# Channel-mixer weight tiles of a two-layer streaming encoder: split up-weights and first and third block sums placed 64 bytes further in longer tiles

## The chip, the core and the metric

The kernel runs on one core of a Trainium2 chip. The metric is the device time of one launch in microseconds (us): the median of several executions, lower is better. A profiled execution on the same core gives the trace from which all shares and durations below come.

## What is computed

The reference is a two-layer encoder over 512 tokens of width 1024 in float32. Layer 0 mixes the tokens with a matrix memory (four heads) and with cross-attention to 256 memory tokens; layer 1 mixes them with chunked band attention (twelve heads) and again with cross-attention. What matters here is the channel mixer that follows in each layer, a gated multilayer perceptron with a causal depthwise convolution of width 3 on its gate, inner width 2816 (22 tiles of 128):

```python
def conv_ffn(h, w_up, conv_w, conv_b, w_down):
    u, g = jnp.split(h @ w_up, 2, axis=-1)
    g = causal_dwconv(g, conv_w, conv_b)
    return (jax.nn.silu(g) * u) @ w_down
...
        x = x + conv_ffn(rmsnorm(x, norm_ffn_g[l]), ffn_w_up[l], ffn_conv_w[l], ffn_conv_b[l], ffn_w_down[l])
```

## The kernel before, in words

Float32 products are made of three matmuls in the float32r type. Every operand is split into a high part (ScalarE, `A.copy`, line 130) and a low part (VectorE, source minus high part, line 131); `mm3` (lines 167 to 171) then multiplies high by high (line 169), high by low (line 170) and low by high (line 171) into one PSUM accumulator. Each of the three is one weight load of 128 by 128 and one matmul over the columns of the other operand. Within `mm3` the stationary operand, the one that is loaded as weights, is mostly a slice of a split weight tile; only the value columns and the last products of the kernel have a split weight tile as the moving operand.

Split weights lie in two rings of three tiles each, `wh` for the high parts and `wl` for the low parts, 128 partitions by 1024 elements (4096 bytes a partition). `parts` (line 148) takes one tile of each ring and splits a raw tile into them; `halves` (line 155) takes the tiles alone. The raw weights come by DMA into the ring `wr`, or, for the gate's weights, into one of two large `pt` tiles. Activations, the split "forms" of this text and much else lie in 57 tiles of 2048 bytes, the ring `u`.

In the program as built, the tiles of `u`, `pt`, `wr`, `t`, `wh` and `wl` all begin 64 bytes past a multiple of 2048 bytes in their partition. A slice of 128 weights takes 512 bytes, and slices of activations begin at halves of their tile (0 or 1024 bytes). So, with a few exceptions, every weight load and every moving operand begins 64 bytes past a multiple of 512. One exception is used below: the value columns of layer 0 (`value_columns(1)`, lines 979 to 1008, called in line 1220) have a moving operand of 392 columns, whose second half begins at 392 times 4 bytes, 32 bytes further with respect to 512. Another is the all-ones weight tile `onesr` (line 103), which begins 128 bytes past a multiple of 512.

A channel mixer (`ChannelMixer`, line 640) does its first five tiles plainly (`plain`, line 676). Its `later` (line 787) does the other 17 in steps that are written out by hand under a manual schedule for TensorE, ScalarE and VectorE (`step`, line 808). A step multiplies 256-column halves of the activations by blocks of the up and gate weights and by sums of such blocks, a scheme that saves block products. The weights of step j+1 are prepared by the class `Forms` (line 854) while step j runs: `sums` and `sum_third` make the block sums in the large tile `mixer.s`, `split_up` (line 889) splits the up weights into `a11` and `a12`, and `split_sums` (line 892) splits the first and third sums into `s1` and `s3`; these two call `parts` and so use `wh` and `wl`. `split_second`, `split_gate` and `split_fourth` put the second sum, a gate block and the fourth sum into `u` tiles; `split_down` (line 899) uses `parts` for the down weights.

In a step, `self.products` (line 766) with `a11`, `a12` and `s1` (lines 828, 831, 839) issues 12 matmuls of 256 columns each. `s3` is used in line 843: in the 12 wide steps of a mixer (j from 9 to 20) by `wide_products` (lines 780 to 785), four pairs of a 256-column matmul with the low part (line 784) and a 512-column matmul with the high part (line 785); in the other five steps by `products`, 12 matmuls of 256 columns. A step's down products (lines 741 to 748) are 512 columns wide and also use `wh` and `wl`.

The order on every engine is the program's: the manual schedule fixes the steps, and the rings `wh` and `wl`, three deep, decide when a split may overwrite an old tile.

Of the kernel before, what the change touches and what calls it, by code (L numbers as in the profile page):

```python
# [10 lines left out]
F32R = mybir.dt.float32r  # L11
# [5 lines left out]
P = 128  # L17
D = 1024
# [37 lines left out]
def trunk(  # L56
# [30 lines left out]
    def sb(tag, shape, dtype=F32):  # L87
        count[0] += 1
        return pool.tile(shape, dtype, tag=tag, name=f"{tag}{count[0]}", bufs=bufs[tag])

    def ps(tag):
        count[0] += 1
        return psum.tile([P, S], F32, tag=tag, name=f"p{tag}{count[0]}", bufs=pbufs[tag])
# [35 lines left out]
    def split(hi, lo, src, on_act=True, pinned=False):  # L129
        high = A.copy(hi, src) if on_act else V.tensor_copy(hi, src)  # L130
        low = V.tensor_tensor(out=lo, in0=src, in1=f(hi), op=ALU.subtract)  # L131
        if pinned:
            pin(high)
            pin(low)
# [10 lines left out]
            nc.sync.dma_start(raw[:, :, b:], extra)  # L145
        return raw

    def parts(raw, pinned=False):
        _, a, b = raw.shape
        hi = sb("wh", [P, D], F32R)[:, : a * b].rearrange("p (a b) -> p a b", a=a)  # L150
        lo = sb("wl", [P, D], F32R)[:, : a * b].rearrange("p (a b) -> p a b", a=a)
        split(hi, lo, raw, pinned=pinned)
        return hi, lo

    def halves(raw):

        _, a, b = raw.shape
        return [sb(tag, [P, D], F32R)[:, : a * b].rearrange("p (a b) -> p a b", a=a) for tag in ("wh", "wl")]

    def weights(*args):  # L160
        return parts(load(*args))

    def rows(w, c0, n, k0=0, k1=None):
        k1 = k1 if k1 is not None else w.shape[0] // P
        return w[k0 * P : k1 * P, c0 : c0 + n].rearrange("(k p) c -> p k c", p=P)
# [85 lines left out]
    class Norm:  # L251
# [14 lines left out]
        def finish(self):  # L266


            parts = [sb("t", [P, S], F32R) for _ in range(2)]
            split(*parts, self.acc)  # L270
            yield 7.4
            o = ps("sc")
            for i, part in enumerate(parts):
                nc.tensor.matmul(o, onesr, part, start=i == 0, stop=i == 1)
            v, r, t = sb("rb", [P, S]), sb("t", [P, S]), sb("t", [P, S])
            A.activation(t, o, AF.Ln, scale=1.0 / D, bias=eps)
            V.tensor_scalar(v, o, 1.0 / D, EPS, op0=ALU.mult, op1=ALU.add)
            A.activation(r, t, AF.Exp, scale=-0.5)
            A.activation(t, r, AF.Square)
            yield 4  # L280
            V.scalar_tensor_tensor(t, t, -0.5, v, op0=ALU.mult, op1=ALU.mult)
            self.row = sb("rb", [P, S])
            V.scalar_tensor_tensor(self.row, t, 1.5, r, op0=ALU.add, op1=ALU.mult)
# [133 lines left out]
    def value_weights(hf, u):  # L417
        n = AW // 2
        ex = rows(a_w_in, 4 * AW, 2 * AH, 2 * u, 2 * u + 2) if hf else None
        return load(rows(a_w_in, 2 * AW + hf * n, n, 2 * u, 2 * u + 2), 2, n, ex)  # L420

    with tc.manual_schedule(engines={mybir.EngineType.PE, mybir.EngineType.Activation, mybir.EngineType.DVE}):
# [9 lines left out]
        for q in range(KT // 2 + 1):  # L432
            if q < KT // 2:
# [6 lines left out]
                hi, lo = sb("u", [P, S], F32R), sb("u", [P, S], F32R)  # L440
# [32 lines left out]
        for j in range(KT):  # L473
            G.dma_start(xspill[j], xT[j])
        norm.spread()
        vws1.append(halves(vraw1[1]))
        A.copy(vws1[1][0], vraw1[1])
        vo = two_banks("mm", "sc")
        value_products(vo, *vws1[0], 0)
        keep(1, 0, ko, A.copy)  # L480
        raw = value_weights(1, 0)
        vw = [halves(raw)]
        A.copy(vw[0][0], raw)
        x_scaled(0)
# [369 lines left out]
    class Forms:  # L854
# [32 lines left out]
            self.sub(self.halves(self.s13)[1], self.halves(self.up)[0], self.halves(self.gate)[0])  # L887

        def split_up(self):
            self.a11, self.a12 = zip(*(self.halves(t) for t in parts(self.up)))  # L890

        def split_sums(self):
            self.s1, self.s3 = zip(*(self.halves(t) for t in parts(self.s13)))

        def sum_fourth(self):
            s2, s4 = self.halves(self.s24)
# [371 lines left out]
    for j in range(KT):  # L1268
        wh, wl = weights(rows(ffn_w_down[0], j * P, P, FT - LAST, FT), LAST, P)
        o = ps("mm")  # L1270
# [175 lines left out]
    for hf in range(2):  # L1446
# [6 lines left out]
        for Ts, pieces in groups:  # L1453
            for c in pieces:
                if c.start:
                    os_[Ts[0]] = ps("mm")
                for u in range(n):
# [3 lines left out]
                    wh, wl = ws[u]  # L1461
# [61 lines left out]
```

## Time and profile before

| | |
|---|---|
| median of 3 runs | 1194.86 us (1194.71 to 1195.16) |
| the profiled execution, its own time | 1195.72 us |
| its span, first to last instruction | 1194.0 us |
| TensorE matmul, busy | 1183.5 us (99%) |
| weight loads, busy (beside the matmuls) | 1037.0 us (87%) |
| VectorE, busy | 961.7 us (81%) |
| ScalarE, busy | 725.2 us (61%) |
| GpSimd, busy | 130.3 us (11%) |
| mean granted TensorE clock | 0.999 |

Matmuls are pipelined, so their durations overlap, and a busy share of 99% says only that there is hardly a moment without one. What a matmul costs is read from the timeline, as the time from one start to the next. `PE` stands for the matmuls, `PEld` for the weight loads, `DVE` for VectorE, `ACT` for ScalarE, `POOL` for GpSimd. A name such as `pmm<-u,wh` gives what is written, then the moving operand, then the weights.

### The profile page before, as it was taken

To read this page: it belongs to the slowest core of one execution; us is meant where nothing else is said; L and a number is where in the kernel's file an instruction comes from. 1 tells how busy PE (TensorE), PEld (TensorE's weight loads), DVE (VectorE), ACT (ScalarE), POOL (GpSimd) and SP (SyncE) were. 2 spreads that over 40 slices of the span, in tenths; PEclk is the share of its full clock that TensorE was granted. 3 is DMA by queue.
4 is the path that set the end of the run, shared out by engine and by line. 5 is a ranking of instruction groups with operands and counts; after the bars stand their busy time and mean duration, and the time that the engine had idled before them with its cause. 6 is when DMAs were issued, how large, how long until landed. Compare 5 with 4: busy or idle time off the path is not lost.

```text
span 1194.0 us, 18184 instructions
## 1 busy us (share of the span) xinstructions
PE 1183.5 (99%) x6719; PEld 1037.0 (87%) x6719; DVE 961.7 (81%) x1760; ACT 725.2 (61%) x1294; POOL 130.3 (11%) x222
## 2 busy tenths in 40 slices
PE   9999999999999999999999999999999999999997
PEld 9988888888899998999888888888889988999986
DVE  6877788788978888888698888997896888888855
ACT  5648677655656555555576677776565655555545
POOL 1211201010021111111020000101001011011100
PEclk9999999999999999999999999999999999999999
DMA  8645313444265676665464313246336455665551
GB/s 289 212 108 140 84 54 80 152 144 141 88 156 147 156 165 165 154 144 123 142 204 123 89 54 101 69 135 185 111 99 141 116 139 135 142 141 139 119 158 71
DMA packets 200155, 158.61 MB, mean 133 GB/s; under 512 B 8344, under 2 KB 179838, under 8 KB 200066
## 3 DMA queue, kind: packets, MB, share of 16 engines
q1 hardware_dynamic: 183906, 119.74, 34.1%
q0 software_dynamic: 15584, 36.67, 14.9%
q8 instruction: 53, 0.87, 0.3%
q10 hardware_dynamic: 576, 1.05, 0.2%
q14 instruction: 36, 0.29, 0.1%
HBM read 128.89 MB, written 32.46 MB: 135 GB/s over the span
## 4 chain that ended last, share of the span: by engine, by line
PE 92%; ACT 3%; DVE 2%; DMA 1%; SPq 1%; issue 0%; POOL 0%; POOLq 0%; DVEq 0%; ACTq 0%
PE pmm L169 15%; PE pmm L170 15%; PE pmm L171 15%; PE ptr L171 6%; PE ptr L169 6%; PE ptr L170 6%; PE pmm L785 6%; PE psc L171 5%; PE psc L170 5%; PE psc L169 5%; PE pmm L784 3%; PE psc L519 2%; PE ptr L1350 1%; DMA wr<-in_mem_w_kv_dram 1%; PE ptr L1371 1%; PE ptr L1372 1%
## 5 line engine op out<-in xcount | busy, mean ns | idle before, releaser
L169 PE MATMUL pmm<-u,wh 128*128 128x512 f32 (+1 forms) x872 | 309.1, 355 | 0.3 <-ACT u L130 0.2
L170 PE MATMUL pmm<-u,wh 128*128 128x512 f32 (+1 forms) x872 | 306.2, 351 | 0.0
L171 PE MATMUL pmm<-u,wl 128*128 128x512 f32 (+1 forms) x872 | 306.0, 351 | 0.0
L131 DVE TENSOR_TENSOR wl<-wr,wh 128x1024 fp32r<-128x1024 f32 (+3 forms) x172 | 199.8, 1163 | 57.0 <-ACT wh L130 55.0
L130 ACT CAST wh<-wr 128x1024 fp32r<-128x1024 f32 (+3 forms) x172 | 172.4, 1004 | 97.7 <-PE pmm L170 44.5
L171 PEld LDWEIGHTS pmm<-u,wl 128*128 128x128 f32 x872 | 164.5, 189 | 21.1
L169 PEld LDWEIGHTS pmm<-u,wh 128*128 128x128 f32 x872 | 164.5, 189 | 18.5 <-ACT u L130 1.1
L170 PEld LDWEIGHTS pmm<-u,wh 128*128 128x128 f32 x872 | 164.7, 189 | 18.2 <-DVE u L131 0.5
L169 PE MATMUL ptr<-u,wh 128*128 128x512 f32 x272 | 106.7, 392 | 0.0
L171 PE MATMUL ptr<-u,wl 128*128 128x512 f32 x272 | 106.1, 390 | 0.0
L753 POOL DMA_DIRECT2D xspill<-t x64 | 55.6, 869 | 461.1 <-ACT t L752 450.4
L170 PE MATMUL ptr<-u,wh 128*128 128x512 f32 x272 | 105.9, 389 | 0.0
L130 ACT CAST u<-pt 128x512 fp32r<-128x512 f32 x102 | 63.0, 620 | 46.8 <-DVE pt L875 46.7
L131 DVE TENSOR_TENSOR u<-pt,u 128x512 fp32r<-128x512 f32 x102 | 69.9, 688 | 11.2 <-ACT u L130 8.5
L169 PE MATMUL psc<-u,wh 128*128 128x256 f32 (+1 forms) x232 | 76.1, 328 | 0.0
L171 PE MATMUL psc<-u,wl 128*128 128x256 f32 (+1 forms) x232 | 75.9, 327 | 0.0
L170 PE MATMUL psc<-u,wh 128*128 128x256 f32 (+1 forms) x232 | 75.9, 327 | 0.0
L937 ACT ACTIVATE t<-t 128x512 f32<-128x512 f32 x34 | 21.6, 634 | 79.3 <-DVE t L660 79.3
L785 PE MATMUL pmm<-u,u 128*128 128x512 f32 x192 | 69.6, 397 | 0.0
L821 DVE TENSOR_TENSOR t<-t,pmm 128x256 f32<-128x256 f32 x72 | 30.2, 419 | 44.9 <-ACT t L819 44.8
L752 ACT COPY t<-ptr 128x512 f32<-128x512 f32 x64 | 37.4, 585 | 43.1 <-PE ptr L171 43.1
L660 DVE SCALAR_TENSOR_TENSOR t<-t,cols,t 128x511 f32<-128x511 f32 x80 | 59.7, 746 | 3.7 <-ACT t L667 3.7
(300 smaller groups left out, 2673.8 us busy)
## 6 DMA issues: line engine op xcount, KB each, us to landing
wr<-in_ffn_w_up_dram SPq DMA_DIRECT2D x54, 512.0 KB, 4.2
wr<-in_ffn_w_down_dram SPq DMA_DIRECT2D x38, 512.0 KB, 4.1
pt<-in_ffn_w_up_dram SPq DMA_DIRECT2D x34, 512.0 KB, 6.2
xspill<-t POOLq DMA_DIRECT2D x64, 256.0 KB, 5.2
wr<-in_a_w_in_dram SPq DMA_DIRECT2D x20, 512.0 KB, 3.7
xspill<-u POOLq DMA_DIRECT2D x32, 256.0 KB, 2.6
u<-xspill SPq DMA_DIRECT2D x32, 256.0 KB, 5.0
wr<-in_w_kv_dram SPq DMA_DIRECT2D x12, 512.0 KB, 3.7
```

The costliest lines, as they stand in the source:

```text
L130: high = A.copy(hi, src) if on_act else V.tensor_copy(hi, src)
L131: low = V.tensor_tensor(out=lo, in0=src, in1=f(hi), op=ALU.subtract)
L169: nc.tensor.matmul(o, lh, rh, start=first, stop=False, skip_group_check=more)
L170: nc.tensor.matmul(o, lh, rl, start=False, stop=False, skip_group_check=more)
L171: nc.tensor.matmul(o, ll, rh, start=False, stop=last, skip_group_check=more)
L519: nc.tensor.matmul(o, a, b, start=first and i == 0, stop=i == 1)
L660: V.scalar_tensor_tensor(acc[:, n:], src[:, : S - n], self.fw[:, c * FT + j : c * FT + j + 1], acc[:, n:], op0=ALU.mult, op1=ALU.add,)
L752: A.copy(t, o)
L753: G.dma_start(xspill[j], t, accum_op=ALU.add)
L784: nc.tensor.matmul(r[:, :H], w[1][:, k], p[i - 1][:, :H], start=False, stop=False, skip_group_check=True)
L785: nc.tensor.matmul(r, w[0][:, k], p[i - 1], start=False, stop=k == n - 1, skip_group_check=True)
L821: V.tensor_tensor(out=o, in0=o, in1=r[:, H:], op=ALU.add)
```

## The change

The tiles of `wh` and `wl` become 64 elements (256 bytes) longer, everywhere in the kernel. `parts` gets an argument `at`, the element at which both split parts begin in their tiles. `split_up` and `split_sums` pass 16, which is 64 bytes; all others pass 0.

```diff
-    def parts(raw, pinned=False):
+    SHIFT = 16
+
+    def weight_tiles(a, b, at=0):
+        places = (at, at)
+        return [
+            sb(tag, [P, D + 64], F32R)[:, o : o + a * b].rearrange("p (a b) -> p a b", a=a)
+            for tag, o in zip(("wh", "wl"), places)
+        ]
+
+    def parts(raw, pinned=False, at=0):
         _, a, b = raw.shape
-        hi = sb("wh", [P, D], F32R)[:, : a * b].rearrange("p (a b) -> p a b", a=a)
-        lo = sb("wl", [P, D], F32R)[:, : a * b].rearrange("p (a b) -> p a b", a=a)
+        hi, lo = weight_tiles(a, b, at)
         split(hi, lo, raw, pinned=pinned)
         return hi, lo
 
     def halves(raw):
 
         _, a, b = raw.shape
-        return [sb(tag, [P, D], F32R)[:, : a * b].rearrange("p (a b) -> p a b", a=a) for tag in ("wh", "wl")]
+        return weight_tiles(a, b)
...
         def split_up(self):
-            self.a11, self.a12 = zip(*(self.halves(t) for t in parts(self.up)))
+            self.a11, self.a12 = zip(*(self.halves(t) for t in parts(self.up, at=SHIFT)))
 
         def split_sums(self):
-            self.s1, self.s3 = zip(*(self.halves(t) for t in parts(self.s13)))
+            self.s1, self.s3 = zip(*(self.halves(t) for t in parts(self.s13, at=SHIFT)))
```

The instructions of each engine, their order and what they wait for stay the same; only addresses differ. The three tiles of `wh` now begin 64, 320 and 576 bytes past a multiple of 2048, those of `wl` 832, 1088 and 1344. The tiles that follow them (`rb`, `bias`) move by 1536 bytes.

## The prediction

> **What bounds the kernel now.** I read the page first: how much of the span has a matmul in it, and what the chain that ended last is made of.
>
> ```profile
> span 1194.0 us, 18184 instructions
> ...
> PE 1183.5 (99%) x6719; PEld 1037.0 (87%) x6719; DVE 961.7 (81%) x1760; ACT 725.2 (61%) x1294; POOL 130.3 (11%) x222
> ...
> PE 92%; ACT 3%; DVE 2%; DMA 1%; SPq 1%; issue 0%; POOL 0%; POOLq 0%; DVEq 0%; ACTq 0%
> ```
>
> TensorE is the chain. The next question is whether it ever waits in the stages that the change touches. I asked the waits view for TensorE alone, and the windows view for the two stretches that hold the steps of the mixers.
>
> ```profile
> PE pmm L428 <- DVE mcf L117: 1.1, 1, 1.1
> PE ptr L392 <- ACT cols L320: 0.9, 1, 0.9
> ...
> PE ptr L169 <- ACT pt L130: 0.2, 1, 0.2
> ```
>
> ```profile
> core 0: us, PE busy (x) PEld busy (x) DVE busy (x) ACT busy (x) POOL busy (x), PEclk, DMA share, GB/s
> 345.00:615.00 270.00, 269.90 (x1708) 244.43 (x1707) 220.38 (x341) 156.95 (x266) 41.29 (x57) 1.00 0.62 154
> 890.00:1135.00 245.00, 245.00 (x1567) 223.10 (x1566) 199.80 (x311) 140.15 (x241) 26.50 (x31) 1.00 0.57 132
> ```
>
> The waits rows are eight, from 1.1 down to 0.2 us, 3.3 us in all. In the two windows TensorE is busy 514.9 of 515 us at a granted clock of 1.00. So nothing that another engine does sets the time there: the mixers last as long as their matmuls follow one another, and only the time from one matmul's start to the next can move the end. I read that from the timeline, in one step.
>
> ```profile
> 449.66 0.39 PE L169 MATMUL ptr<-u,wh 128*128 128x512 f32 x1
> ...
> 451.70 0.28 PE L784 MATMUL pmm<-u,u 128*128 128x256 f32 x1
> 451.81 0.40 PE L785 MATMUL pmm<-u,u 128*128 128x512 f32 x1
> 452.05 0.28 PE L784 MATMUL pmm<-u,u 128*128 128x256 f32 x1
> 452.16 0.40 PE L785 MATMUL pmm<-u,u 128*128 128x512 f32 x1
> 452.40 0.28 PE L784 MATMUL pmm<-u,u 128*128 128x256 f32 x1
> 452.52 0.40 PE L785 MATMUL pmm<-u,u 128*128 128x512 f32 x1
> 452.76 0.28 PE L784 MATMUL pmm<-u,u 128*128 128x256 f32 x1
> 452.87 0.40 PE L785 MATMUL pmm<-u,u 128*128 128x512 f32 x1
> ```
>
> ```profile
> 454.54 0.28 PE L169 MATMUL pmm<-u,wh 128*128 128x256 f32 x1
> ...
> 457.42 0.28 PE L784 MATMUL pmm<-u,u 128*128 128x256 f32 x1
> ```
>
> From 449.66 to 451.70 lie 9 matmuls of 512 columns: 2.04/9 = 226.7 ns each. From 454.54 to 457.42 lie 24 of 256 columns, the products with `a11` and `a12`: 2.88/24 = 120.0 ns each. The difference, 106.7 ns for 256 columns, is the streaming; what is left, 120.0 - 106.7 = 13.3 ns, is the same for both widths. It is a fixed price that each load-and-matmul pair pays, and the only thing on this path that a new address could change. It isn't quite fixed: the four 256-column matmuls that follow a 512-column one take 0.11, 0.11, 0.12 and 0.11 us to the next start, 112.5 on average, a fixed part of 5.8 ns.
>
> **The change part by part.** No instruction is added, removed or moved on any queue; no wait changes. Three things get new addresses.
>
> First, the shifted weight loads. By the loops, each step has 36 matmuls of 256 columns with `a11`, `a12` and `s1`; over 2 mixers of 17 steps that is 34 x 36 = 1224. `s3` gives 12 more in each of the 10 narrow steps (120), and four pairs in each of the 24 wide ones (96 of 256 and 96 of 512 columns). So 1440 of 256 columns and 96 of 512, 1536 in all, read their weights 64 bytes further; their moving operands stay. The trace shows no sustained stream of matmuls with weights at such a place, so the cost has to be bounded. Below: the fixed part falls from 13.3 to the 5.8 ns of the rows above, 7.5 ns each, 1536 x 7.5 = 11.5 us less. Above: it doubles, 1536 x 13.3 = 20.4 us more. Between these ends I look for the row that is nearest to a shift of one operand against the other, and find the value columns of layer 0: 392 columns, weights at 64 past a multiple of 512 throughout, the moving operand at 64 in one group of 12 and at 96 in the next.
>
> ```profile
> 40.66 0.34 PE L169 MATMUL pmm<-wh,u 128*128 128x392 f32 x1
> ...
> 42.79 0.34 PE L169 MATMUL pmm<-wh,u 128*128 128x392 f32 x1
> ...
> 44.92 0.34 PE L169 MATMUL pmm<-wh,u 128*128 128x392 f32 x1
> ...
> 47.06 0.34 PE L169 MATMUL pmm<-wh,u 128*128 128x392 f32 x1
> ...
> 49.19 0.34 PE L169 MATMUL pmm<-wh,u 128*128 128x392 f32 x1
> ```
>
> The group from 40.66 has its moving operand at 64, that from 42.79 at 96, and so on in turn: 2.13, 2.13, 2.14 and 2.13 us. A shift of 32 bytes between weights and moving operand costs less than 0.01 us in 12 matmuls. A second near row is the load of the all-ones tile, which begins where the shifted slices will lie (128 past a multiple of 512, in one ring place of two):
>
> ```profile
> L244 PEld LDWEIGHTS psc<-t,onesr x10: 186/188/192, 30.0 to 248.6; 128*128 128x128 f32 x10
> ```
>
> ```profile
> L785 PEld LDWEIGHTS pmm<-u,wh 128*128 128x128 f32 x96 | 18.1, 189 | 3.4
> ```
>
> Its load lasts 188 ns in the median, the loads that the change shifts 189 in the mean. I take 0 for this part: both near rows say that a load and a matmul don't ask where they begin. Its ends, -11.5 and +20.4 us, are kept for the range.
>
> Second, the longer tiles. The middle one of `wh` and two of `wl` now begin 256 bytes off their former place with respect to 512, and with them about half of the 512-column loads of the plain tiles, the down products and the projections. The same reasoning holds, and the same value, 0. If places mattered by 256 bytes as well, this part would count with the sign of the first; I can't bound it apart from that.
>
> Third, the splits write and read at the new places: 68 copies on ScalarE and 68 subtractions on VectorE.
>
> ```profile
> L131 DVE TENSOR_TENSOR wl<-wr,wh 128x1024 fp32r<-128x1024 f32 x143 | 174.9, 1223 | 49.2 <-ACT wh L130 47.3
> ...
> L131 DVE TENSOR_TENSOR u<-t,u 128x512 fp32r<-128x512 f32 x62 | 42.7, 689 | 4.2 <-ACT u L130 4.1
> ...
> L131 DVE TENSOR_TENSOR pt<-ptr,pt 128x512 fp32r<-128x512 f32 x28 | 19.1, 686 | 3.1 <-ACT pt L130 3.1
> ```
>
> A subtraction with two operands in SBUF, both at the same place in their 512 bytes, takes 689 ns; with one of them in PSUM 686 (the splits into `wl` are the same operation, 1223 ns for 1024 elements). So two reads at one place don't disturb each other now, and moving one of them can't win anything. Could it lose? One step's window shows the cover:
>
> ```profile
> 451.70:467.16 15.46, 15.46 (x98) 13.94 (x97) 12.76 (x21) 8.73 (x15) 2.94 (x4) 1.00 0.66 159
> ```
>
> VectorE is busy 12.76 of 15.46 us, and two of its shifted subtractions fall into a step. With 2.7 us free, each would have to lose over 1.3 us, more than its own 1.22, before VectorE became the bound. ScalarE has 6.7 us free. I take 0; if that cover were gone, the excess over 1.3 us would count twice a step, 34 times.
>
> Where the second group of 256-column matmuls stands against the notes: the Trainium skill, page "TensorE: Matmul & The Clock Gate", section "Back-to-back issue gap", gives N/2.4 + 2.5 ns between warm matmuls, which is an estimated 109.2 ns at 256 columns; the rows here show 120.0, 10.8 more, so the trace doesn't agree. By that page, if the whole excess came from where the weights lie and the shift removed it, the estimate would be 1536 x 10.8 = 16.6 us less, 1178.3 us. The same page, under "Step-by-step: what each phase is for", says that loading the next weights takes no read bandwidth from the running matmul; no run here shows that for other weight places, and by it the sum stays 0.
>
> The sum: 0 + 0 + 0 on the profiled execution's 1195.72 us (span 1194.0 and 1.7 around it). That execution lay 0.86 above the median of the runs shown, so for the median I predict 1194.9.
>
> **The rivals.** Faster: the fixed part is a collision of two readings. A weight load starts with the matmul before it, so both read SBUF at once.
>
> ```profile
> 451.70 0.19 PEld L785 LDWEIGHTS pmm<-u,u 128*128 128x128 f32 x1
> ...
> 452.05 0.19 PEld L785 LDWEIGHTS pmm<-u,u 128*128 128x128 f32 x1
> ```
>
> The loads of line 785 start at 451.70 and 452.05, the very times of line 784's matmuls above. If their common beginning at 64 past 512 is what costs, and a shift parts them, 7.5 ns go from each: 1194.9 - 11.5 = 1183.4. For it: the fixed part isn't the same everywhere (5.8 against 13.3). Against it: the 392-column groups, and that the fixed part is equally large over hundreds of pairs whose tiles lie anywhere.
>
> Slower: a matmul takes a column each 0.417 ns (106.7/256) and its load, spread over the 120 ns of the pair, a weight each 0.94 ns, so the moving read runs about twice as fast. Begun at one place, it is ahead from the first moment. Weights that begin 64 bytes ahead (320 in a tile that the longer ring moves) are overtaken once in each load; if readings at one place block each other, each pair pays for it. Half of the fixed part again, 6.7 ns, gives 1536 x 6.7 = 10.3 us, 1205.2; the whole of it 1215.3. It decides from about 1.6 ns a pair (2.4 us over 1536). Against it stand the same 392-column rows, though there the moving operand was put ahead, which would not bring an overtaking.
>
> That the change does something else than it says: only the longer tiles matter, through the 512-column loads. That is the first or the second rival with another number of pairs, and I count it with them.
>
> **How the numbers follow.** No change, 1194.9: 0.52. Faster, about 1183: 0.22. Slower, about 1205: 0.26. A change of 0.2%, 2.4 us, is about the least that a measurement of this kernel can tell from none, so same is 1192.5 to 1197.3. Both rivals hold much chance, because weights at another place are never seen in a stream here. The range of the likeliest case alone is 1193.5 to 1196.5. The whole range, 1186 to 1207, takes in all of that, the lesser half of the faster rival (0.11 is left out below) and somewhat more than half of the slower one (0.09 left out above).
>
> **What the changed profile would show.** If I am right, 24 matmuls with `a11` and `a12` still take 2.88 us from first to last start, a step 15.46 us, and line 784 with `wl` keeps its pattern. The faster rival shows 112 to 118 ns in such a group, the slower one 124 to 133, and products with weights in `u` tiles (the second and fourth sums), whose places don't change, stay at 120. If only the longer tiles matter, the down products leave 226.7 ns while `a11` stays. Subtractions of line 131 into `wl` off 1223 ns by more than 1% would show the third part wrong, without a move of the end. What would make the prediction wrong is any such change of TensorE's pace; no wait can, since none is near.

## The result, and the profile after

The changed kernel takes **1190.38 us** (median of 6 runs, 1189.69 to 1191.35), the kernel before 1194.86 in 6 runs beside it: a ratio of 0.9962, 95% interval 0.995 to 0.9975. That is 4.5 us less. The prediction said no change, 1194.9; the time lies in its whole range (1186 to 1207) and outside that of its likeliest case (1193.5 to 1196.5). The profiled execution took 1191.35 us.

The page of the changed kernel, at the places shown of before:

```profile
span 1189.6 us, 18184 instructions
...
PE 1179.0 (99%) x6719; PEld 1032.1 (87%) x6719; DVE 961.9 (81%) x1760; ACT 723.6 (61%) x1294; POOL 130.0 (11%) x222
...
PE 92%; ACT 3%; DVE 2%; DMA 2%; issue 0%; SPq 0%; POOL 0%; POOLq 0%; DVEq 0%; ACTq 0%
```

As many instructions as before, and the same chain. The span is 4.4 us shorter, and so is the busy time of the matmuls (4.5): the time left from inside TensorE's stream, not from a wait. The windows view of the same two stretches says where:

```profile
core 0: us, PE busy (x) PEld busy (x) DVE busy (x) ACT busy (x) POOL busy (x), PEclk, DMA share, GB/s
345.00:615.00 270.00, 269.90 (x1719) 244.04 (x1719) 222.64 (x344) 157.74 (x267) 41.38 (x58) 1.00 0.63 155
890.00:1135.00 245.00, 245.00 (x1583) 222.88 (x1582) 201.76 (x311) 140.78 (x241) 27.29 (x32) 1.00 0.58 133
```

TensorE was full before and is full now, at the same granted clock of 1.00, but 1719 and 1583 matmuls fit where 1708 and 1567 did. The timeline of the step that the prediction read (line numbers are 8 higher now, so 177 to 179 are the three matmuls of `mm3`, and 792 and 793 the pair of `wide_products`):

```profile
453.90 0.28 PE L179 MATMUL psc<-u,u 128*128 128x256 f32 x1
454.02 0.28 PE L177 MATMUL pmm<-u,wh 128*128 128x256 f32 x1
...
456.75 0.28 PE L792 MATMUL pmm<-u,u 128*128 128x256 f32 x1
```

The 24 products with `a11` and `a12` take 456.75 - 454.02 = 2.73 us, 113.8 ns each, where it was 2.88 and 120.0. The fourth sum's products ahead of them, whose weights lie in `u` and did not move, keep their 0.12 us. A whole step, from the first product of the gate block (`a22`, whose low and high parts alternate 256 and 512 columns) to the next step's, has become shorter by about as much (15.30 against 15.45 us):

```profile
451.17 0.28 PE L792 MATMUL pmm<-u,u 128*128 128x256 f32 x1
...
466.47 0.28 PE L792 MATMUL pmm<-u,u 128*128 128x256 f32 x1
```

Not every shifted product gained so much. Those with `s1` come right behind the 512-column down products:

```profile
460.90 0.28 PE L177 MATMUL psc<-u,wh 128*128 128x256 f32 x1
...
462.32 0.28 PE L792 MATMUL pmm<-u,wl 128*128 128x256 f32 x1
```

1.42 us for 12, 118 ns each. And the same `a11` and `a12` products gain only 2 ns in a step that follows a narrow one, where the gate block's products have 256 columns and nothing alternates ahead of them:

```profile
380.01 0.28 PE L177 MATMUL pmm<-u,wh 128*128 128x256 f32 x1
...
382.84 0.28 PE L177 MATMUL pmm<-u,u 128*128 128x256 f32 x1
```

2.83 us for 24, 117.9 ns each. Taking the time from each of the 6719 matmuls to the next, and adding it up by kind of pair in both traces, gives the whole account:

| pairs | before, ns | after, ns | gained, us |
|---|---|---|---|
| 576 of 256 columns: `a11`, `a12` in the 24 steps that follow a wide one | 120.0 | 114.0 | 3.4 |
| 240 of 256 columns: `a11`, `a12` in the other 10 steps | 119.9 | 117.9 | 0.5 |
| 120 of 256 columns: narrow `s3` | 120.0 | 118.0 | 0.2 |
| 408 of 256 columns: `s1` | 119.6 | 117.8 | 0.7 |
| 96 of 256 columns: wide `s3` | 117.7 | 118.1 | 0.0 |
| 96 of 512 columns: wide `s3` | 235.6 | 234.2 | 0.1 |
| 1044 of 256 columns, weights and moving operand in `u` | 120.7 | 120.9 | -0.2 |

The shifted 256-column pairs give 4.85 us together; small losses elsewhere leave 4.4.

### The profile page after: what moved, and what is told of

Read it like the earlier page. It is cut to its first block, busy times and chain, and to the rows that moved or that the text cites. A ratio compares the mean times of both kernels' runs of the same rounds, so it can differ in the third digit from the quotient of the medians.

```text
span 1189.6 us, 18184 instructions
## 1 busy us (share of the span) xinstructions
PE 1179.0 (99%) x6719; PEld 1032.1 (87%) x6719; DVE 961.9 (81%) x1760; ACT 723.6 (61%) x1294; POOL 130.0 (11%) x222
## 4 chain that ended last, share of the span: by engine, by line
PE 92%; ACT 3%; DVE 2%; DMA 2%; issue 0%; SPq 0%; POOL 0%; POOLq 0%; DVEq 0%; ACTq 0%
PE pmm L177 15%; PE pmm L178 15%; PE pmm L179 14%; PE ptr L178 6%; PE ptr L177 6%; PE ptr L179 6%; PE pmm L793 6%; PE psc L179 5%; PE psc L178 5%; PE psc L177 5%; PE pmm L792 3%; PE psc L527 2%; DMA wr<-in_mem_w_kv_dram 2%; PE ptr L1358 1%; PE ptr L1379 1%; PE ptr L1380 1%
## 5 line engine op out<-in xcount | busy, mean ns | idle before, releaser
L177 PE MATMUL ptr<-u,wh 128*128 128x512 f32 x272 | 106.7, 392 | 0.0
```

Of the source, the lines that this page charges most:

```text
L177: nc.tensor.matmul(o, lh, rh, start=first, stop=False, skip_group_check=more)
```

## The experiments

**Theories.** The distance theory: a load and the matmul that runs beside it disturb each other by how far apart their places are, so the pace of a pair depends on the place of the weights *relative to* the moving operand, and 0 was a bad distance at 256 columns. Its rivals: the longer tiles move half of the plain weights by 256 bytes, and that is the gain; or the absolute place counts (64 past 512 is bad for anything). The first three runs part these.

**Only the longer tiles.**

```diff
-    SHIFT = 16
+    SHIFT = 0
```

> The longer tiles alone, nothing shifted: every weight slice begins at 64 past a multiple of 256 bytes, in half of the tiles 256 bytes off with respect to 512. Theory A (a weight load is dearer when it does not begin at a multiple of 128 bytes) and theory B (a load and the moving operand collide when both begin at the same place with respect to 64 or 128 bytes) both expect the time of before, 1194.9 us, and 120 ns between matmuls of 256 columns. Theory C (the longer tiles brought the gain, through distances of 256 bytes) expects the 1190.4 us of the changed kernel.

Measured: 1195.21 us, ratio 1.0003 (0.9994 to 1.0012). In its timeline the `a11` and `a12` products are back at the pace of before:

```profile
453.25 0.28 PE L177 MATMUL pmm<-u,wh 128*128 128x256 f32 x1
...
456.13 0.28 PE L792 MATMUL pmm<-u,u 128*128 128x256 f32 x1
```

2.88 us for 24. The longer tiles alone change nothing that the interval could show; the 64 bytes make the gain.

**Everything moved alike.** The kernel before with a tile of 64 bytes ahead of the rings, so that split weights and moving operands both begin at multiples of 128 bytes and their distances stay (a few constant tiles ahead of it, such as `onesr`, keep their places).

```diff
+    pad = cpool.tile([P, 16], F32, name="pad")
+    V.memset(pad, 0.0)
```

> The kernel before with 64 bytes of padding ahead of all its tiles: every tile then begins at a multiple of 128 bytes, the distance between weights and moving operands is as before. Theory A expects a gain on every stream with 256 columns, those with weights in u tiles too: 1188 us or less. Theory B expects no change, 1194.9 us.

Measured: 1194.89 us, ratio 0.9999 (0.9991 to 1.0008). Moving both by 64 bytes does not count. Of the three theories the distance is left.

**All split weights shifted.** If 64 bytes are good for the mixers' 256-column pairs, are they good for all?

```diff
-    def weight_tiles(a, b, at=0):
+    def weight_tiles(a, b, at=SHIFT):
...
-    def parts(raw, pinned=False, at=0):
+    def parts(raw, pinned=False, at=SHIFT):
```

> Every split weight tile begins 64 bytes further, not only the up-weights and the two sums. If the gain holds for every width (theories A and B), some 2000 loads with 512 columns and the plain tiles' products gain too: at 3 ns each about 6 us more, 1184 us. If only 256-column streams gain, where the load nearly fills the time between two matmuls, the time stays within 1 us of the changed kernel's 1190.4. The value columns, where the split tile is the moving operand, tell little here.

Measured: 1202.39 us, ratio 1.0059 (1.0046 to 1.0071): slower, which neither of the two expectations had. The down products, 512 columns each, now have shifted weights too. Their timeline:

```profile
447.17 0.39 PE L177 MATMUL ptr<-u,wh 128*128 128x512 f32 x1
...
449.27 0.39 PE L177 MATMUL ptr<-u,wh 128*128 128x512 f32 x1
```

Nine take 2.10 us, 233.3 ns each, where distance 0 gave 226.7. Over the trace the 2832 pairs of 512 columns with weights in `wh` or `wl` lose 12.9 us and the 256-column pairs gain 6.3; the balance of 6.6 is most of the 7.3 measured (against 1195.07 of the runs beside it). So the same shift wins at one width and loses at the other, and the change gains because it shifts almost only the narrow pairs.

**The pace by itself.** A kernel with nothing but streams of 36 pairs, one accumulator each, weights and moving operand at chosen places:

```python
for i in range(COUNT):
    a = (6 * ROW if i % 3 == 2 else 2 * ROW) + weight_bytes // 4 + i // 3 % 8 * P
    b = (10 + i % 7 * 2) * ROW + moving_bytes // 4
    nc.tensor.matmul(o[:, :n], big[:, a : a + P], big[:, b : b + n], start=i == 0, stop=i == COUNT - 1)
```

> Leaves out the whole computation: it runs streams of 36 load-and-matmul pairs, one stream for each choice of width, place of the weights (w for the two high parts, l for the low part of each three) and place of the moving operand (m, and k for the second of each three), in bytes past a multiple of 2048. With 256 columns and weights and moving operand at 64 it should show the 120 ns of before. Theory A: about 113 ns wherever the weights begin at 0, 128, 256 or 384, whatever m is; 120 at 64, 192, 320 and 448. Theory B: 113 ns wherever w and m differ by an odd multiple of 64, for m at 0, 64 and 128 alike; 120 where they are equal, at w 0 with m 0 and w 128 with m 128 too. The streams of 384 and 512 columns show whether longer matmuls gain as well (226.7 ns at 512 before).

The timeline puts a stream in one row: its start, its length to the end of its last matmul, and a name made of the columns (n), the weights' place (w, l) and the moving operand's (m, k) in bytes. The pace is the time from one row's start to the next, divided by 36.

```profile
27.23 4.48 PE L53 MATMUL n256w64l64m64k64x<-big 128*128 128x256 f32 x36
31.55 4.42 PE L53 MATMUL n256w80l80m64k64x<-big 128*128 128x256 f32 x36
...
44.30 4.25 PE L53 MATMUL n256w128l128m64k64x<-big 128*128 128x256 f32 x36
48.39 4.44 PE L53 MATMUL n256w144l144m64k64x<-big 128*128 128x256 f32 x36
...
69.76 4.47 PE L53 MATMUL n256w320l320m64k64x<-big 128*128 128x256 f32 x36
74.07 4.41 PE L53 MATMUL n256w384l384m64k64x<-big 128*128 128x256 f32 x36
78.31 4.44 PE L53 MATMUL n256w448l448m64k64x<-big 128*128 128x256 f32 x36
...
150.38 8.35 PE L53 MATMUL n512w64l64m64k64x<-big 128*128 128x512 f32 x36
158.56 8.33 PE L53 MATMUL n512w80l80m64k64x<-big 128*128 128x512 f32 x36
...
175.12 8.56 PE L53 MATMUL n512w128l128m64k64x<-big 128*128 128x512 f32 x36
183.52 8.53 PE L53 MATMUL n512w192l192m64k64x<-big 128*128 128x512 f32 x36
```

At 256 columns, distance 0: (31.55 - 27.23)/36 = 120.0 ns, as in the kernel before. Distance 64: (48.39 - 44.30)/36 = 113.6, and 113.3 once the first eight pairs are left out. Distance 256 (weights at 320, moving at 64): 119.7, as slow as 0, so 256 bytes are as good as none; that fits the longer tiles' doing nothing. At 512 columns distance 0 is the good one (227.2), and 64 costs 233.3. No other engine works beside these streams, so the kernel's other traffic has no part in it. One thing did not fit: distance 320, the same as 64 by a period of 256, gave (78.31 - 74.07)/36 = 117.8, and so did 64 bytes with the moving operand at 0 or at 128; two streams that mix weights at 128 and 384 gave 113.9 and 113.3. 64 bytes know two paces, about 113.3 and 117.8, the two that `a11` and `s1` show in the kernel.

**Behind 512 columns.** The same streams, finer in distance, each behind nine pairs of 512 columns, as `s1` stands in the kernel.

> Leaves out the whole computation, as the first streams did. Each stream of 36 pairs now comes behind 9 pairs with 512 columns at 64 and 64, as in the mixers, so that no stream inherits the pace of the one before. Theory B with a period of 256 bytes (distance d = place of the weights minus place of the moving operand): d = 0, 256 and 512 at 120.0 ns with 256 columns. For d = 64 the first streams showed two paces, 113.3 and 117.8. If the pace is inherited, each place has one pace here and always the same: 113.3 at d = 64 and the mixture 128/384, as the kernel's up-weights show, and 117.8 where the moving operand alternates between 64 and 1088, as its first sums show. If it is chance, the mixture differs from what the kernel shows. Rival: the pace depends on the place itself and not on the distance, then d = 576-64 = 512 need not equal d = 0. With 512 columns: 226.7 at d = 0, 16, 192 and 256, 232 to 234 at 64; distances just below 256 are unknown, by symmetry with d = 16 about 226.7.

```profile
66.39 4.40 PE L50 MATMUL n256w128l128m64k64x<-big 128*128 128x256 f32 x36
70.63 2.24 PE L57 MATMUL between<-big 128*128 128x512 f32 x9
...
85.34 4.26 PE L50 MATMUL n256w140l140m64k64x<-big 128*128 128x256 f32 x36
89.44 2.24 PE L57 MATMUL between<-big 128*128 128x512 f32 x9
```

Now 64 bytes give (70.63 - 66.39)/36 = 117.8, and so do the streams that mix weights at 128 and 384, for which 113.3 was expected; so what ran before has a say. Distance 76 gives 113.9, the best of this run; those around it (72 and 80) give 118.3 and 118.6. At 512 columns 16 and 240 bytes are as good as 0 (226.7), 8 and 248 are not (230.7 and 233.3). The dependence is a jagged one, and no rule was found that says which distance is good.

**One half of the split each.** Only the high parts shifted, then only the low parts (two of three pairs, and one of three).

```diff
-        places = (at, at)
+        places = (at, 0)
```

```diff
-        places = (at, at)
+        places = (0, at)
```

> Only the high parts begin 64 bytes further, the low parts stay at the start of their (longer) tiles. By the streams with weights at 128, 128, 64 a pair takes 117.8 ns instead of the 113.3 of the up-weights in the changed kernel: 816 pairs with a11 and a12 gain 2.2 instead of 6.7 ns, 1.8 us instead of 5.4. Theory B expects 1192 to 1194 us, between before and the change. If what counts is the write or the read of the splits (the two parts at one place), it expects the 1190.4 of the change or the 1194.9 of before.

> Only the low parts begin 64 bytes further. By the streams with weights at 64, 64, 128 the same 117.8 ns: theory B expects 1192 to 1194 us here too. The high weights of the 512-column matmuls in the wide products stay unshifted, so it should be a little faster than the run with the high parts shifted, by up to 96 x 6 ns = 0.6 us.

Measured: 1192.06 us (ratio 0.9974, 0.9964 to 0.9984) and 1192.51 (0.998, 0.9972 to 0.9989). The low parts' run was expected to be a little faster than the high parts'; it isn't, and the intervals don't part the two. By the traces the products with `a11`, `a12` and `s1` take 117.8 or 117.9 ns a pair in both: about 2 ns gained by each of some 1340 pairs is 2.8 us, the gain that the high parts' run shows. Shifting one pair in three is worth nearly as much as two in three, so the price isn't one that each pair pays for its own distance: streams in which only some pairs are shifted settle at the slower of the two paces of 64 bytes; in none of them was the faster seen.

**Only the up-weights.** `split_sums` without the shift.

```diff
-            self.s1, self.s3 = zip(*(self.halves(t) for t in parts(self.s13, at=SHIFT)))
+            self.s1, self.s3 = zip(*(self.halves(t) for t in parts(self.s13)))
```

> Only the up-weights are shifted, the first and third sums stay. Theory B: a11 and a12 keep 113.3 to 113.6 ns a pair (816 pairs, 5.4 us gained), s1 and s3 go back to 120 (about 2 ns each on 528 pairs and the wide pairs, 1 to 1.5 us lost against the change): 1191 to 1192 us. If the gain needs both (a pace that is carried on from one group to the next), the up-weights lose their 113 too and the time is over 1193 us.

Measured: 1191.18 us, ratio 0.9971 (0.996 to 0.9981). The up-weights alone bring 3.7 of the 4.5 us; the sums bring the rest, too little to tell from nothing by the time alone, though the trace has it (`s1` back at 119.6 ns).

**Two leads.** Streams of 24 pairs at 24 distances, each behind 12 pairs of 512 columns, and behind these and 12 more of 256 columns, to see whether the narrow pairs ahead of `a11` make the faster pace.

> Leaves out the whole computation. Each of 24 distances from 52 to 248 bytes between weights and moving operand is run twice with 24 pairs of 256 columns, once behind 12 pairs of 512 columns and once behind 12 pairs of 256 columns at distance 0, the leads that the first sums and the up-weights have in the changed kernel. If the pace is inherited from the lead, distance 64 isn't in the list of ties: it shows 117.8 behind 512 columns and 113.3 behind 256. If the two paces at distance 64 were chance, both leads show the same. At distance 76 both leads should reach 113.3, by the stream with weights at 140; other distances 117 to 120. A rival: any distance that isn't a multiple of 16 bytes pays for it, so 113.3 appears at 64, 80 and 96 only.

```profile
64.55 2.99 PE L46 MATMUL n256w128l128m64k64x<-big 128*128 128x256 f32 x24
67.38 2.91 PE L53 MATMUL wide<-big 128*128 128x512 f32 x12
...
71.55 2.99 PE L46 MATMUL n256w128l128m64k64x<-big 128*128 128x256 f32 x24
74.38 2.92 PE L53 MATMUL wide<-big 128*128 128x512 f32 x12
...
102.33 2.90 PE L46 MATMUL n256w140l140m64k64x<-big 128*128 128x256 f32 x24
105.06 2.91 PE L53 MATMUL wide<-big 128*128 128x512 f32 x12
...
109.24 2.89 PE L46 MATMUL n256w140l140m64k64x<-big 128*128 128x256 f32 x24
111.97 2.92 PE L53 MATMUL wide<-big 128*128 128x512 f32 x12
```

64 bytes: 2.83/24 = 117.9 behind either lead. So narrow pairs ahead of it are not what makes `a11` fast. 76 bytes: 2.73/24 = 113.8 behind both. Of the other distances none is that fast behind both; once settled, 52 and 168 are so behind the second lead alone, 88 behind the first alone.

**76 bytes in the kernel.** A distance that doesn't ask what ran before should lift `s1` as well.

```diff
-    SHIFT = 16
+    SHIFT = 19
```

> As the change, but 76 bytes instead of 64. If 113.3 ns at 76 holds behind both leads, the first and the third sums of the narrow steps gain 4.5 ns more on some 500 pairs: about 2 us less than the change, 1188 us. If the streams with alternating moving operands (64 and 1088) don't reach that pace, the sums stay near 118 and the time is that of the change, 1190 to 1191. If 76 bytes only found 113.3 by its lead, the up-weights go to 118 and the time is 1193.

Measured: **1187.83 us**, ratio 0.9943 (0.993 to 0.9957), faster than both kernels. Its `a11` and `a12` group:

```profile
451.85 0.28 PE L177 MATMUL pmm<-u,wh 128*128 128x256 f32 x1
...
454.60 0.28 PE L792 MATMUL pmm<-u,u 128*128 128x256 f32 x1
```

2.75/24 = 114.6 ns; over the trace `a11`, `a12` and narrow `s3` take 114.6 and `s1` 114.5, where 64 bytes left `s1` at 117.8. 936 x 5.4 + 408 x 5.1 = 7.1 us, which is the gain. What it has over 64 bytes comes from `s1`, the narrow `s3` and the `a11` and `a12` of the 10 steps without alternation (113.8 instead of 117.9); in the other 24 steps it is 0.7 ns a pair dearer (114.7 against 114.0).

**Other widths.** Streams of 192 to 512 columns at distances 0, 64 and 76, and the prediction's own row: 392 columns with the moving operand at 64 and at 96.

> Leaves out the whole computation. First the case on which the prediction took its 0: 392 columns with weights at 64 and moving operand at 64 and 96 should repeat 177.7 ns for both. If that width never reacts, weights at 96, 128 and 140 show 177.7 too; if only that one distance, 32 bytes backwards, was harmless, they show 180 or more, and 256 columns with the moving operand at 96 stay at 120. Then widths from 192 to 448 at distances 0, 64 and 76: 384 and 512 columns lost by 64 bytes (3.4 and 6.7 ns) where 256 gained. If the gain belongs to matmuls that end while the next load is still being read, it should be there up to about 256 to 272 columns and turn into a loss from 288 on.

```profile
29.84 6.54 PE L48 MATMUL n392w64l64m64k64x<-big 128*128 128x392 f32 x36
36.22 2.23 PE L55 MATMUL between<-big 128*128 128x512 f32 x9
38.28 6.56 PE L48 MATMUL n392w64l64m96k96x<-big 128*128 128x392 f32 x36
44.68 2.24 PE L55 MATMUL between<-big 128*128 128x512 f32 x9
...
72.22 4.47 PE L48 MATMUL n256w64l64m64k64x<-big 128*128 128x256 f32 x36
76.53 2.23 PE L55 MATMUL between<-big 128*128 128x512 f32 x9
78.60 4.36 PE L48 MATMUL n256w64l64m96k96x<-big 128*128 128x256 f32 x36
82.80 2.23 PE L55 MATMUL between<-big 128*128 128x512 f32 x9
...
103.09 4.17 PE L48 MATMUL n224w64l64m64k64x<-big 128*128 128x224 f32 x36
107.11 2.24 PE L55 MATMUL between<-big 128*128 128x512 f32 x9
```

The moving operand 32 bytes further: 177.2 to 177.8 ns at 392 columns, a loss of 0.6; 119.7 to 116.7 at 256 columns, a gain of 3.0. The row was read rightly, and stands for that one distance at its own width: with the weights 76 bytes further, 392 columns take 179.8. A gain up to 272 columns and a loss from 288 on was expected. At 64 bytes 272 columns gain 1.9 ns, 288 lose 1.4 and 384 lose 2.5, but 320 and 448 change by less than 0.4, so width alone doesn't give the sign either. At 224 columns a pair takes 4.02/36 = 111.7 ns, and 192 and 128 columns settle there as well, at every distance tried: up to about 240 columns the pace doesn't depend on the columns, so most likely the weight load sets it, though no run changes the load. 256 columns stream in 106.7 ns, 5 less than that floor, so the two limits lie close together there.

**Many leads.** Which history makes 64 bytes fast? Twelve leads, among them nearly a copy of what stands ahead of `a11` in the kernel behind a wide step: nine pairs of 512 columns (twelve in the kernel), four alternations of 256 and 512, twelve of 256.

> The kernel's computation is left out; only streams of load-and-matmul pairs are run. Each is 24 pairs of 256 columns, moving operand at 64 bytes past a multiple of 512, with the weights 64 bytes further (streams named behind) or 76 bytes further (named far), and each comes behind one of twelve leads at distance 0: 9 pairs of 512 columns, then none or four alternations of a 256- and a 512-column pair (that is what stands ahead of the fourth sums in the kernel), then 0 to 36 pairs of 256 columns, one lead with 36 pairs of 256 columns at distance 48; all of them twice. Open is why the products with the up-weights ran at 113.8 ns a pair behind the 256-column products of the fourth sums while the same stream ran at 117.7 behind 12 pairs of 256 columns. If the history of the pairs alone chooses the pace, the lead that copies the kernel (nine wide, four alternations, twelve narrow) gives 113.3 to 114 ns at 64 bytes, both times, and the leads divide into some with 113.3 and some with 117.8. If something else in the kernel chooses it (traffic of other engines, the place of the result), all leads give 117 to 118 at 64 bytes. By either, 76 bytes gives 113 to 114 behind every lead.

```profile
29.99 2.90 PE L45 MATMUL behind_a__145<-big 128*128 128x256 f32 x24
...
36.21 2.90 PE L45 MATMUL behind_b__190<-big 128*128 128x256 f32 x24
...
42.43 2.99 PE L45 MATMUL behind_c__238<-big 128*128 128x256 f32 x24
...
109.73 2.99 PE L45 MATMUL behind_l__754<-big 128*128 128x256 f32 x24
```

A stream's length here holds the last matmul's own 0.28 us; without it, over 23 starts, 2.90 is 114 ns a pair and 2.99 is 118. The copy of the kernel (a) gives the fast pace, the alternations alone (b) too, and the same with one narrow pair more; the lead without alternations (c) gives the slow one, and so do the seven others without them. Four alternations and 24 narrow pairs (l) give the slow one again. All repeat within half a nanosecond the second time, and 76 bytes stay at 113.3 to 114.8 behind all twelve. So the history of the pairs, by itself and the same each time, chooses between the two paces: `a11` is fast where the wide products of the gate block, narrow and wide in turn, ran 12 narrow pairs earlier. The kernel's own trace bears that out: 114.0 ns in the 24 steps with such a block ahead, 117.9 in the 10 without. Behind pairs of 512 columns it doesn't hold: the second sum's alternations stand ahead of `s1` too, but 12 such pairs lie between, and `s1` is slow. Nor are alternations the only such history: in the first streams 64 bytes were fast behind 36 pairs at 48 bytes, while the same 36 pairs behind nine wide ones (lead j) give the slow pace. How the alternations hand the pace on through 12 pairs which run at 120 ns themselves stays open.

## Why the prediction was wrong, point by point

**The bound** was right: TensorE alone, at a full clock, so only the time from one start to the next could move the end. All of the 4.5 us came from there.

**The fixed part** of 13.3 ns was right as the place to look. It is not a fixed price, but depends on the distance: 113.3 to 120 ns at 256 columns is a fixed part of 6.6 to 13.3. The 5.8 that the prediction took from the narrow matmuls of an alternating stream as its lower end was nearly what a good distance reaches.

**The shifted loads** are the step that failed: "I take 0 for this part: both near rows say that a load and a matmul don't ask where they begin." Neither row was near. The 392-column groups were a shift of another size (32 bytes, not 64) at another width, and the width matters: the same 32 bytes cost 0.6 ns there and gain 3.0 at 256 columns. The load of `onesr` gave a duration (188 ns) that is longer than the pair's whole pace of 120, since loads overlap too; it doesn't show the pace. A row that could have warned stood in the same part: the alternating stream, where the same kind of pair paid 5.8 ns, showed that the fixed part does depend on circumstances. In place of 0 the runs show about 3.4 ns gained on each of the 1440 shifted pairs of 256 columns, 4.85 us in all, and 0.1 us for the 96 of 512.

**The longer tiles** at 0 were right (1195.21 without the shift), though not for the reason given, and so by luck: places do matter, but 256 bytes more cost as much as none (120.0 and 119.7 ns). **The splits** at 0 were right too; the two groups of line 131 into `wl` that hold the shifted splits stand at 1223 and 1220 ns, as they did before:

```profile
L131 DVE TENSOR_TENSOR wl<-wr,wh 128x1024 fp32r<-128x1024 f32 x143 | 174.9, 1223 | 49.1 <-ACT wh L130 47.3
...
L131 DVE TENSOR_TENSOR wl<-pt,wh 128x1024 fp32r<-128x1024 f32 x34 | 41.5, 1220 | 1.5 <-ACT wh L130 1.5
```

**The faster rival** was the one that happened, at less than half of its price: a beginning at one place costs 6.0 ns in `a11` and `a12` behind alternations, 2.0 in the other steps and 1.8 in `s1`, not 7.5 everywhere. That two readings of the memory collide, as it has it, no run shows. Its argument against itself, that the fixed part is equally large over hundreds of pairs whose tiles lie anywhere, was weak: tiles anywhere, but all at 64 past 512, so all at one distance. Its sign test for the after profile (112 to 118 ns for the group, 120 for the products with weights in `u`) is what the trace shows. **The slower rival** has the right sign for 512 columns (226.7 to 233.3, e.g. the down products with everything shifted), which the change leaves alone. Its picture of weights being overtaken was not tested.

**The estimate beside the sum.** That from the Trainium skill, page "TensorE: Matmul & The Clock Gate", section "Back-to-back issue gap", was an estimated 109.2 ns at 256 columns, by a formula that the section gives for the gap of a single matmul, without a budget for the load. No run with loads reaches it: the best stream of 256 columns stands at 113.3, and shorter ones settle at 111.6 or more. Under "Step-by-step: what each phase is for" the same page of the Trainium skill says that loading the next weights takes no read bandwidth from the running matmul. The streams show that load and matmul do get in each other's way somehow, since the pace of the same loads and matmuls changes with nothing but the distance of their addresses (113.3 to 120.0 ns). Whether they meet in reading the memory or elsewhere, no run here shows.

## What to carry to other kernels

Where TensorE is full, the price of a load-and-matmul pair is a matter of addresses too: take the pace from a stream of the very width, at several distances between weights and moving operand, before calling it fixed. Choose the distance for each width by itself (here 76 bytes for 256 columns, 0 for 512), since a shift that gains at one width loses at another, and prefer one whose pace doesn't ask what ran before. And a row is near only if it agrees in what the effect may hang on: width, distance, and what ran before.

## What the runs showed of the hardware that was not expected

- The pace of float32r pairs goes with the distance between weights and moving operand, without a rule that these runs could find: 113.3 to 120 ns at 256 columns, 226.7 to 234.2 at 512. 0, 256 and 512 bytes are alike at 256 columns (119.7 to 120.0), which speaks for a period of 256. Moving both operands by 64 bytes made no difference (1194.89 against 1194.9 us).
- From 128 to about 240 columns a float32r pair settles at 111.6 to 112.2 ns at every distance tried, whatever its width.
- The same stream at one distance (64 bytes) has two steady paces, 113.3 and 117.8 ns, and what ran before chooses between them: alternating pairs of 256 and 512 columns up to 13 narrow pairs earlier bring the faster one, and behind 24 narrow pairs their effect is gone.
